# A decoder layer with two head groups: values of the delta rule turned in 32x32 blocks by VectorE, placed by four stores, and scaled by GpSimd after the scan's load

## The chip, the cores and the metric

The kernel runs on one core of one Trainium2 chip, as one launch, in 32-bit floats. The metric is device time in microseconds (us). Before the change the median of three runs is 1235.05 us (1234.37 to 1235.09). The engines are named as the profile names them: PE is TensorE's matmul, PEld its weight load, DVE VectorE, ACT ScalarE, POOL GpSimd, SP SyncE, which issues most of the DMAs.

## What is computed

One decoder layer for 1024 tokens of width 1024. One projection feeds two head groups that work in parallel: group A is differential attention (4 heads), group B a gated delta rule (4 heads, keys and values of 128). Both outputs go through one output projection, and an MLP follows. The change touches the values `v` of group B alone:

```python
dn_qkv = causal_conv_silu(dn_qkv, conv_w[l])
dn_q, dn_k, dn_v = jnp.split(dn_qkv, [DN_HEADS * DN_K_DIM, 2 * DN_HEADS * DN_K_DIM], axis=-1)
...
v_beta = v * beta[..., None]
...
u, w = sol[..., :Dv], sol[..., Dv:]
def step(state, inp):
    q_c, k_c, u_c, w_c, qk_c, g_c = inp
    v_new = u_c - jnp.einsum('bhcd,bhde->bhce', w_c, state)
    o = (jnp.einsum('bhcd,bhde->bhce', q_c * jnp.exp(g_c)[..., None], state)
         + jnp.einsum('bhcj,bhje->bhce', qk_c, v_new))
    ...
```

In words: a causal convolution and SiLU make q, k and v; a triangular system inside each chunk couples the tokens; a scan over chunks carries a 128x128 state for each head.

## The kernel before

All large matmuls are made in three products of rounded halves (hH, hL for the normed input, wH, wL for the weights). The time up to about 350 us runs in these stages.

**Values, keys, queries of the delta rule** (`dn_proj`, L666, up to about 245 us). For each kind (keys, then queries, then values), each head h and each half hf of 512 tokens, TensorE makes a projection `ps_dn` with channels on the partitions and tokens along the free dimension (24 matmuls), ScalarE copies it to `cp`, ScalarE and VectorE do the convolution (`cy`), ScalarE the SiLU. `skew` delays the consumer by one item, so that the next projection is issued first.

The scan wants tokens on the partitions. For the values (loop at L851) `transposed` (L713) therefore sends the four 128x128 tiles of an item through TensorE into PSUM (`ps_t`, L716); VectorE multiplies them by a factor for each token and head (`vsc`, L854) while it moves them to `kn`; `park` (L701) stores the 512x128 result to the DRAM tensor `park_d`, slot 2, in one DMA on SP's queue. `park_d` holds five slots for each head, chunk of 128 tokens and token: raw keys, scaled keys, values, queries and the masked q-k products. The factor `vsc` is made earlier, with the keys (L787, GpSimd).

**The inverse of the triangular system** (`invert`, L743, and `horner`, L797). VectorE inverts 32x32 blocks and sends them through DRAM (`fsg_d`); `horner` loads them into `gb` (L804, sixteen small DMAs for a pair of heads), turns them with a 32x32 block transpose on VectorE (L806), and combines blocks with matmuls `ps_p` (L810) and `ps_h` (L818); `pb` (L813) is a masked copy between them. It is called four times in the value loop, each for a pair of heads and a half.

**The scan** (`scan`, L902), from about 249 to 345 us, interleaved with the projections of group A. It goes through eight chunks. `load` (L907) fetches slots 0 to 2 of a chunk for the four heads into `pka`, four DMAs on SP's queue (L910); `pka` has two buffers, so chunks 0 and 1 are loaded at once and each later load waits until the chunk two before it has been read. `sr` (L922) is values minus keys times state, for chunk 0 the values themselves; then come a matmul with the inverse (L930), a copy `sy` (L932), the state's update (L941, L947) and, in `scan_out` (L956), the chunk's output, which needs slots 3 and 4 (`pkb`, L960).

**Queries, keys and values of group A** (`da_units`, L1041, `da_turns`, L1020) run on TensorE in the same time, one 128-token unit after the other: 24 matmuls `ps_qk` (L1067 to L1069), a norm whose power -1/2 is taken by GpSimd (`rstd`, L288, `rn` at L291), the product `qn` on VectorE (L1092), two transposes `ps_qkt` (L1028, L1029), and a store `qk_d` issued from GpSimd's queue (L1034). When the keys of two heads are stored, `load_head` fetches them (`KS`, L1118) on SP's queue.

**What sets the order.** Within `manual_schedule` and the `Interleave` planner the streams are merged at build time by estimated durations; the tile framework then fixes one order for each engine's queue, also from estimates. On the chip every queue is strictly in order: an instruction that waits for a semaphore holds all that stands behind it on its engine. The same goes for SP's queue of DMAs.

The lines that the change and the prediction touch: the value loop L851 to L857, `park` L701, `load` L907 and its use at L913 and L933; and, beside them on GpSimd's queue, L291, L991 (`mixn_d`), L1034.

Of the kernel before, what the change touches and what calls it, by code (L numbers as in the profile page):

```python
# [13 lines left out]
ALU = mybir.AluOpType  # L14
# [8 lines left out]
NT = SEQ // P  # L23
# [84 lines left out]
def act(n, accum=False):  # L108
    return "S", 55.0 + 0.83 * n + (93.0 if accum else 0.0)


def vec(n, extra=0.0):
    return "V", 68.0 + 1.045 * n + extra


def powr(n):
    return "G", 180.0 + 285.0 * n
# [3 lines left out]
def tile_hymba_layer(  # L121
# [6 lines left out]
    nc = tc.nc  # L128
    V, S, G, T = nc.vector, nc.scalar, nc.gpsimd, nc.tensor
# [40 lines left out]
    park_d = dram.tile([HEADS, NT, P, 5, P], F32, name="park_d")  # L170
# [117 lines left out]
    def rstd(o, ss, scale, eps, pool, tag, n):  # L288
        t = pool.tile([P, n], F32, tag=tag, name=tag) if pool else laid(tag)
        V.tensor_scalar(t, ss, scale, eps, ALU.mult, ALU.add)  # L290
        G.tensor_tensor(o, t, neghalf[:, :n], ALU.pow)  # L291
# [187 lines left out]
    with tc.manual_schedule(engines={T.engine, V.engine, S.engine, G.engine}):  # L479
# [49 lines left out]
        for tb in range(3, NT):  # L529
            for u in range(2):  # L530
                nxt, at = spread_at.get((tb, u), (None, 0))
                z[tb, u] = z_mm(tb, u, *pools[tb], nxt, at)
                if nxt is not None:
# [4 lines left out]
                    if nxt in (4, 5):  # L538
                        b = {4: 5, 5: 7}[nxt]
# [32 lines left out]
    ps = ph.tile([P, 512], F32, tag="ph", name="ps_pv")  # L572
# [24 lines left out]
    v4 = lambda t: t.rearrange("p (c d) -> p c d", d=P)  # L597
# [37 lines left out]
    ps = ph.tile([P, 512], F32, tag="ph", name="ps_g")  # L635
# [21 lines left out]
    def ta(name, bufs, dt=F32):  # L657
        return sa.tile([P, 512], dt, tag=name, name=name, bufs=bufs)

    ssq, ssk, rq, bp, kds, vsc = smalls + [sp.tile([P, 32], F32, name=n) for n in ("kds", "vsc")]  # L660
# [32 lines left out]
    def skew(gen):  # L693
        prev = None
        for it in gen:
            if prev is not None:
                yield prev
            prev = it
        yield prev

    def park(h, hf, slot, src):  # L701
        nc.sync.dma_start(park_d[h, 4 * hf:4 * hf + 4, :, slot, :].rearrange("c p d -> p c d"), v4(src))

    def cols4(t, h, hf):
        return t[:, 8 * h + 4 * hf:8 * h + 4 * hf + 4]

    def bc_col(t):
        return t.unsqueeze(2).broadcast_to([P, 4, P])
# [4 lines left out]
    def transposed(src):  # L713
        ps = pt_.tile([P, 512], F32, tag="pt", name="ps_t")
        for c in range(4):
            T.transpose(ps[:, c * P:(c + 1) * P], src[:, c * P:(c + 1) * P], ident)  # L716
        return ps
# [41 lines left out]
    for h, hf, y, th in skew(dn_proj(1)):  # L759
# [3 lines left out]
        ps = transposed(k2)  # L763
# [65 lines left out]
    for h, hf, q2 in skew(dn_proj(0)):  # L829
# [3 lines left out]
        ps = transposed(q2)  # L833
# [15 lines left out]

    heads = [((h, h + 1), hf) for hf in range(2) for h in (0, 2)]  # L850
    for h, hf, v2 in skew(dn_proj(2)):  # L851
        ps = transposed(v2)
        vs = ta("kn", 2)
        V.tensor_tensor(v4(vs), v4(ps), bc_col(cols4(vsc, h, hf)), ALU.mult)  # L854
        park(h, hf, 2, vs)
        if hf == 0:
            horner(*heads.pop(0))  # L857

# [43 lines left out]
    def scan():  # L902
        St = {}
        psA = pA.tile([P, 512], F32, name="ps_A")
        PA = {h: psA[:, h * P:(h + 1) * P] for h in range(HEADS)}

        def load(c):  # L907
            pka = sb.tile([P, HEADS, 3, P], F32, tag="pka", name="pka", bufs=2)
            for h in range(HEADS):
                nc.sync.dma_start(pka[:, h], park_d[h, c, :, 0:3, :])  # L910
            return pka

        nxt = load(0)  # L913
        for c in range(NT):
            pk, rr_, yy = nxt, {}, {}
            if c > 0:
                for h in range(HEADS):
                    T.matmul(PA[h], pk[:, h, 0, :], St[h], start=True, stop=True)
                for h in range(HEADS):
                    i = cidx(h, c)  # L920
                    rr_[h] = sb.tile([P, P], F32, tag="sr", name="sr", bufs=4)
                    V.scalar_tensor_tensor(rr_[h], PA[h], neg_eg[:, i:i + 1], pk[:, h, 2, :], ALU.mult, ALU.add)  # L922
                flow.pe(4 * MM)
                yield flow.chain(*[vec(P, 60)] * 4), None
            else:
                for h in range(HEADS):
                    rr_[h] = pk[:, h, 2, :]
            for h in range(HEADS):
                Wc = W[h, c // 4][:, (c % 4) * P:(c % 4 + 1) * P]
                T.matmul(PA[h], Wc, rr_[h], start=True, stop=True)  # L930
            y4 = sb.tile([P, 512], F32, tag="sy", name="sy", bufs=2)
            S.copy(y4, psA)  # L932
            if c + 1 < NT:  # L933
                nxt = load(c + 1)
            flow.pe(4 * MM)
            yield flow.chain(act(512)), None
            Sold = dict(St)
            for h in range(HEADS):
                yy[h] = y4[:, h * P:(h + 1) * P]
                if c < NT - 1:  # L940
                    T.matmul(PA[h], pk[:, h, 1, :], yy[h], start=True, stop=True)  # L941
            if c < NT - 1:
                for h in range(HEADS):
                    i = cidx(h, c)
                    Sn = sb.tile([P, P], F32, tag=f"S{h}", name=f"S{h}", bufs=2)
                    if c > 0:
                        V.scalar_tensor_tensor(Sn, St[h], elast[:, i:i + 1], PA[h], ALU.mult, ALU.add)  # L947
                    else:
                        V.tensor_copy(Sn, PA[h])
                    St[h] = Sn  # L950
                flow.pe(4 * MM)
            flow.add(1, scan_out(c, Sold, yy), 0, "pB")
            if c < NT - 1:
                yield flow.chain(*[vec(P, 60)] * 4), None

    def scan_out(c, Sold, yy):  # L956
        pkb = {}
        for h in range(HEADS):
            pkb[h] = sb.tile([P, 2, P], F32, tag="pkb", name="pkb", bufs=5)
            nc.sync.dma_start(pkb[h], park_d[h, c, :, 3:5, :])  # L960
        zgt = sb.tile([P, 512], F32, tag="zgt", name="zgt", bufs=1)
        nc.sync.dma_start(zgt, zg_d[c])
        oc = sb.tile([P, 512], F32, tag="oc", name="oc", bufs=2)
        so = sb.tile([P, 4], F32, tag="so", name="so", bufs=2)
        osq = sb.tile([P, P], F32, tag="osq", name="osq", bufs=1)
        yield flow.now + 2500, "pB"
        if c > 0:
            o1 = pB.tile([P, 512], F32, tag="pB", name="ps_o1")
            for h in range(HEADS):
                T.matmul(o1[:, h * P:(h + 1) * P], pkb[h][:, 0, :], Sold[h], start=True, stop=True)  # L970
            V.tensor_tensor(v4(oc), v4(o1), bc_col(eg[:, c::8]), ALU.mult)
            flow.pe(4 * MM)
            flow.hold("pB", flow.chain(vec(512)))
            yield flow.now, "pB"
        o2 = pB.tile([P, 512], F32, tag="pB", name="ps_o2")
        for h in range(HEADS):
            T.matmul(o2[:, h * P:(h + 1) * P], pkb[h][:, 1, :], yy[h], start=True, stop=True)
        if c > 0:
            V.tensor_tensor(oc, oc, o2, ALU.add)
        else:  # L980
            S.copy(oc, o2)
        for h in range(HEADS):
            i = cidx(h, c)
            S.activation(osq, oc[:, h * P:(h + 1) * P], AF.Square, scale=rq[:, i:i + 1], accum_out=so[:, h:h + 1])
        f = sb.tile([P, 4], F32, tag="of", name="of", bufs=2)
        rstd(f, so, 1.0 / P, EPS, sb, "oft", 4)
        V.tensor_tensor(f, f, rq[:, c::8], ALU.mult)
        for h in range(HEADS):
            V.scalar_tensor_tensor(oc[:, h * P:(h + 1) * P], oc[:, h * P:(h + 1) * P], f[:, h:h + 1],
                                   zgt[:, h * P:(h + 1) * P], ALU.mult, ALU.mult)  # L990
        nc.gpsimd.dma_start(mixn_d[c], oc)  # L991
        flow.pe(4 * MM)
        t = flow.chain(vec(512))
        flow.hold("pB", t)
        flow.chain(*[act(P, True)] * 4, vec(4), powr(4), vec(4), *[vec(P, 60)] * 4, start=t)
        if c == NT - 1:
            s2ctx.close()
            spctx.close()
            mp = ctx.enter_context(tc.tile_pool(name="mp", bufs=1, **left))
            pools["mp"] = mp  # L1000
            for tb in tiles:
                accs[tb] = row_tile("acc")
            pools["a2"] = bctx.enter_context(tc.tile_pool(name="a2", bufs=1, **left))
            pools["be"] = bctx.enter_context(tc.tile_pool(name="be", bufs=2, **left))
            pools["rsc"] = scctx.enter_context(tc.tile_pool(name="rsc", bufs=1, space=PSUM, **right))
            state["scan"] = True
# [911 lines left out]
```

## Time and profile before

| | before |
|---|---|
| median of three runs | 1235.05 us |
| profiled execution | 1234.74 us |
| its span (first to last instruction) | 1233.0 us |
| TensorE busy | 1217.3 us (99%) |
| VectorE busy | 824.7 us (67%) |
| ScalarE busy | 624.2 us (51%) |
| GpSimd busy | 151.3 us (12%) |
| bytes moved by DMA | 202.12 MB |

How to read the rows that follow. A row of a group is: line, engine, operation, out<-in with shapes, count, then busy us and mean ns of one, then the idle time of the engine just before it and what ended it. A row of the timeline is: start in us from the span's start, duration in us, engine (a q behind it is the engine's queue), line, operation, count. A row of a window is: the stretch, its length, then the busy us of PE, PEld, DVE, ACT and POOL with their counts, the granted clock of TensorE, the share of the DMA engines and GB/s. A row of the chain of waits is: start, duration, what. Rows of DMA issues give the KB of each and the median us from issue to landing. Matmul durations overlap, so the cost of one in a stream is read from the distance of the starts.

### The profile page before, as it was taken

What the parts mean: (1) busy time and instruction counts of PE and PEld (TensorE: products, weight loads), DVE (VectorE), ACT (ScalarE), POOL (GpSimd) and SP (SyncE); (2) the same over time, 40 slices, a digit from 0 to 9 for tenths busy, and PEclk for the clock granted to TensorE, in tenths of its full rate; (3) what the DMA queues carried; (4) which work ended last, traced back from release to release, by engine and by line L of the source; (5) the groups of instructions that cost most, each with busy time, mean ns of one, the idle gap of its engine ahead of it and who ended that gap; (6) DMA issues with size and microseconds to landing.
All of it is one profiled execution on the core that took longest, in us unless ns stands there. A gap on an engine that the chain in (4) does not pass through costs nothing.

```text
span 1233.0 us, 18819 instructions
## 1 busy us (share of the span) xinstructions
PE 1217.3 (99%) x6823; PEld 1054.3 (86%) x6823; DVE 824.7 (67%) x1524; ACT 624.2 (51%) x1249; POOL 151.3 (12%) x215
## 2 busy tenths in 40 slices
PE   9999999999999999999999999999999999999998
PEld 8978888898999998888888888888888888888886
DVE  6868796556647657777799544565569755777543
ACT  6588553344346555566666544444564333333330
POOL 2411110043434421001200000000000000000000
PEclk9999999999999999999999999999999999999999
DMA  9344653278748756323437434444479645423301
GB/s 350 98 115 122 163 162 104 63 234 240 231 148 252 232 162 159 85 77 108 157 117 255 172 122 151 171 170 153 155 241 382 234 179 184 163 103 103 137 35 69
DMA packets 143301, 202.12 MB, mean 164 GB/s; under 512 B 20920, under 2 KB 98280, under 8 KB 143208
## 3 DMA queue, kind: packets, MB, share of 16 engines
q1 hardware_dynamic: 138584, 187.28, 46.9%
q0 software_dynamic: 4480, 13.64, 2.9%
q8 instruction: 54, 0.88, 0.3%
q14 instruction: 39, 0.32, 0.1%
q10 hardware_dynamic: 144, 0.00, 0.0%
HBM read 135.86 MB, written 65.01 MB: 163 GB/s over the span
## 4 chain that ended last, share of the span: by engine, by line
PE 88%; DVE 4%; DMA 3%; ACT 2%; issue 2%; POOL 1%; SPq 1%; POOLq 0%; DVEq 0%; ACTq 0%
PE X L1517 4%; PE X L1515 4%; PE X L1516 4%; PE X L1814 4%; PE X L1815 4%; PE X L1813 4%; PE ps_dn L265 3%; PE ps_dn L267 3%; PE ps_dn L266 3%; PE ps_qk L1067 3%; PE ps_qk L1068 3%; PE ps_qk L1069 3%; PE ps_o L1250 2%; PE Y L1515 2%; PE Y L1517 2%; PE Y L1516 2%
## 5 line engine op out<-in xcount | busy, mean ns | idle before, releaser
L1433 ACT CAST hH<-ur 128x1024 fp32r<-128x1024 f32 x56 | 58.9, 1051 | 173.4 <-PE Y L1814 89.8
L1434 DVE TENSOR_TENSOR hL<-ur,hH 128x1024 fp32r<-128x1024 f32 x56 | 68.3, 1223 | 79.4 <-ACT hH L1433 79.4
L1067 PE MATMUL ps_qk<-wH,hH 128*128 128x256 f32 x384 | 114.3, 298 | 0.0
L1069 PE MATMUL ps_qk<-wH,hL 128*128 128x256 f32 x384 | 108.7, 283 | 0.0
L1068 PE MATMUL ps_qk<-wL,hH 128*128 128x256 f32 x384 | 108.4, 282 | 0.0
L1434 DVE TENSOR_TENSOR op<-raw,op 128x1024 fp32r<-128x1024 f32 x48 | 58.7, 1223 | 74.2 <-PE X L1516 41.1
L1813 PE MATMUL X<-hH 128*128 128x512 f32 x224 | 87.1, 389 | 0.0
L1814 PE MATMUL X<-hL,hH 128*128 128x512 f32 x224 | 87.1, 389 | 0.0
L1815 PE MATMUL X<-hH,hL 128*128 128x512 f32 x224 | 87.1, 389 | 0.0
L265 PE MATMUL ps_dn<-hH,wH 128*128 128x512 f32 x192 | 76.3, 397 | 0.2 <-ACT cp L678 0.2
L267 PE MATMUL ps_dn<-hH,wL 128*128 128x512 f32 x192 | 75.8, 396 | 0.0
L266 PE MATMUL ps_dn<-hL,wH 128*128 128x512 f32 x192 | 75.8, 395 | 0.0
L1068 PEld LDWEIGHTS ps_qk<-wL,hH 128*128 128x128 f32 x384 | 73.4, 191 | 0.2
L1067 PEld LDWEIGHTS ps_qk<-wH,hH 128*128 128x128 f32 x384 | 73.3, 191 | 0.2
L1069 PEld LDWEIGHTS ps_qk<-wH,hL 128*128 128x128 f32 x384 | 73.1, 190 | 0.0
L1434 DVE TENSOR_TENSOR hL<-dw,hH 128x1024 fp32r<-128x1024 f32 x56 | 68.2, 1218 | 0.9 <-ACT hH L1433 0.9
L1433 ACT CAST op<-raw 128x1024 fp32r<-128x1024 f32 x48 | 50.4, 1052 | 35.7 <-PE Y L1517 19.9
L1433 ACT CAST hH<-dw 128x1024 fp32r<-128x1024 f32 x56 | 58.7, 1048 | 10.7 <-DMA dw<-in_w_down_dram 5.0
L1205 ACT ACTIVATE pexp<-pexp,mx 128x128 f32<-128x128 f32 (+7 forms) x64 | 49.7, 777 | 25.1 <-DVE mx L1204 24.5
L682 DVE SCALAR_TENSOR_TENSOR cy<-cp,pv,cy 128x512 f32<-128x512 f32 x72 | 53.7, 747 | 8.1 <-ACT cy L680 7.3
L1340 PE MATMUL ps_op<-wH,hH 128*128 128x512 f32 x128 | 53.0, 414 | 0.0
L1515 PE MATMUL Y<-hH,op 128*128 128x512 f32 x128 | 49.9, 390 | 0.4 <-DVE ua L1555 0.4
(370 smaller groups left out, 3429.1 us busy)
## 6 DMA issues: line engine op xcount, KB each, us to landing
ur<-ud SPq DMA_DIRECT2D x28, 1024.0 KB, 5.0
raw<-in_w_up_dram SPq DMA_DIRECT2D x32, 512.0 KB, 3.9
dw<-in_w_down_dram SPq DMA_DIRECT2D x32, 512.0 KB, 6.8
wraw<-in_w_units_dram SPq DMA_DIRECT2D x48, 256.0 KB, 3.7
qk_d<-qa POOLq DMA_DIRECT2D x32, 256.0 KB, 4.3
ud<-ua SPq DMA_DIRECT2D x16, 512.0 KB, 4.2
ud<-s SPq DMA_DIRECT2D x16, 512.0 KB, 2.7
pka<-park_d SPq DMA_DIRECT2D x32, 192.0 KB, 4.8
```

The source lines that it names most:

```text
L265: T.matmul(ps, lh(k), rh(k), start=(k == 0), stop=False)
L266: T.matmul(ps, lh(k), rl(k), start=False, stop=False)
L267: T.matmul(ps, ll(k), rh(k), start=False, stop=(k == n - 1))
L1067: T.matmul(ps[:, :256], hH[:, k, sl], wh[:, k, :], start=(k == 0), stop=False)
L1068: T.matmul(ps[:, :256], hH[:, k, sl], wl[:, k, :], start=False, stop=False)
L1069: T.matmul(ps[:, :256], hL[:, k, sl], wh[:, k, :], start=False, stop=(k == KB - 1))
L1433: S.copy(dst[0], src)
L1434: V.tensor_tensor(dst[1], src, dst[0].bitcast(F32), ALU.subtract)
L1515: T.matmul(ps, op[0][:, k, cs], h[0][:, k, :], start=start and k == 0, stop=False, skip_group_check=True)
L1813: T.matmul(bank[t], v[0][:, j, sl], v[2][:, j], start=s0, stop=False, skip_group_check=True)
L1814: T.matmul(bank[t], v[0][:, j, sl], v[3][:, j], start=False, stop=False, skip_group_check=True)
L1815: T.matmul(bank[t], v[1][:, j, sl], v[2][:, j], start=False, stop=s1, skip_group_check=True)
```

## The change

The values no longer go through TensorE. VectorE turns `v2` in blocks of 32x32 within the 128x512 tile (`V.transpose`), which puts tokens on partitions inside each block but leaves the blocks at their place; four DMAs (`put_blocks`), one for each group of 32 channels, write the blocks to where they belong in `park_d`, in runs of 32 floats. The factor `vsc` is no longer applied there. Instead GpSimd multiplies slot 2 of `pka` by it, in place, after a chunk has been loaded: chunk 0 ahead of the loop, chunk c + 1 at the end of chunk c.

```diff
+    def put_blocks(dst, src):
+
+        for a in range(4):
+            s = slice(32 * a, 32 * a + 32)
+            nc.sync.dma_start(dst[:, s].rearrange("(b s) r -> s b r", s=32),
+                              src[s].rearrange("s (b r) -> s b r", r=32))
...
     for h, hf, v2 in skew(dn_proj(2)):
-        ps = transposed(v2)
         vs = ta("kn", 2)
-        V.tensor_tensor(v4(vs), v4(ps), bc_col(cols4(vsc, h, hf)), ALU.mult)
-        park(h, hf, 2, vs)
+        V.transpose(vs, v2)
+        put_blocks(park_d[h, 4 * hf:4 * hf + 4, :, 2, :].rearrange("c p d -> (c p) d"), vs)
...
+        def scale(c, pk):
+            G.tensor_tensor(pk[:, :, 2, :], pk[:, :, 2, :], bc_col(vsc[:, c::8]), ALU.mult)
+
         nxt = load(0)
+        scale(0, nxt)
         for c in range(NT):
...
             flow.add(1, scan_out(c, Sold, yy), 0, "pB")
+            if c + 1 < NT:
+                scale(c + 1, nxt)
             if c < NT - 1:
                 yield flow.chain(*[vec(P, 60)] * 4), None
```

In the order of the built programs TensorE's queue loses the 32 transposes, and the steps of `horner` stand at other places among the projection matmuls; from the scan's first matmul on, the order on TensorE, VectorE and ScalarE is as before, but for one product `qn` on VectorE that changes places with its neighbour. GpSimd's queue has the eight scalings among its other instructions, SP's has 24 DMAs more.

## The prediction

> **What bounds the kernel now.** I read the head of the page first, then its chain of waits, then the busy time by stretches of 20 us around the two places that the change touches: the values of the delta rule are made from about 185 to 245 us, and the scan loads them from 249 to 320 us.
>
> ```profile
> PE 1217.3 (99%) x6823; PEld 1054.3 (86%) x6823; DVE 824.7 (67%) x1524; ACT 624.2 (51%) x1249; POOL 151.3 (12%) x215
> PE 88%; DVE 4%; DMA 3%; ACT 2%; issue 2%; POOL 1%; SPq 1%; POOLq 0%; DVEq 0%; ACTq 0%
> 200.00:220.00 20.00, 20.00 (x131) 16.62 (x131) 13.88 (x23) 7.99 (x17) 0.00 (x0) 1.00 0.44 117
> 280.00:300.00 20.00, 17.75 (x149) 17.26 (x149) 12.23 (x42) 7.87 (x26) 9.18 (x11) 1.00 0.88 256
> 300.00:320.00 20.00, 19.18 (x166) 18.99 (x165) 13.97 (x42) 9.87 (x31) 6.95 (x9) 1.00 0.83 260
> ```
>
> TensorE is busy 99% of the span and holds 88% of the chain. From 200 to 220 us it has no gap (20.00 of 20.00, granted clock 1.00). So a matmul taken out there is time saved, and a wait put in front of a matmul anywhere is time lost: the order on TensorE is fixed when the kernel is built, and nothing fills the hole. VectorE (13.88 of 20) and GpSimd (0.00 there, 9.18 of 20 in the scan) have room by their busy time. In the scan the DMA engines are the crowded part (0.83 to 0.88).
>
> **What the change takes away.** Eight times four transposes through TensorE (L716 for the values).
>
> ```profile
> 188.67 0.39 PE L266 MATMUL ps_dn<-hL,wH 128*128 128x512 f32 x1
> 188.90 0.39 PE L267 MATMUL ps_dn<-hH,wL 128*128 128x512 f32 x1
> 189.13 0.60 PE L716 MATMUL ps_t<-ident,k 128*128 128x128 f32 x4
> 189.49 0.47 PE L265 MATMUL ps_dn<-hH,wH 128*128 128x512 f32 x1
> 189.80 0.39 PE L266 MATMUL ps_dn<-hL,wH 128*128 128x512 f32 x1
> ```
>
> Undisturbed projection matmuls start 0.23 us apart (188.67, 188.90, 189.13). With the four transposes between, the starts go 189.13, 189.49, 189.80: 0.67 us for what takes 0.23, so a group costs 0.44 us. Eight groups: **-3.5 us**.
>
> **What it puts on VectorE and SP before the scan.**
>
> ```profile
> L854 DVE TENSOR_TENSOR kn<-ps_t,vsc 128x512 f32<-128x512 f32 x8 | 5.4, 678 | 2.6 <-PE ps_t L716 2.6
> L806 DVE STREAM_TRANSPOSE W<-gb 128x512 f32<-128x512 f32 x8 | 5.6, 703 | 1.5 <-DMA gb<-fsg_d 1.4
> L813 DVE TENSOR_TENSOR pb<-ps_p,blk 128x384 f32<-128x384 f32 x8 | 4.3, 541 | 7.5 <-PE ps_p L810 7.5
> q1 hardware_dynamic: 2016, 0.34, 22.2%
> gb<-fsg_d SPq DMA_DIRECT2D x14, 16.0 KB, 1.9
> park_d<-kn SPq DMA_DIRECT2D x16, 256.0 KB, 2.3
> 233.97 9.08 SPq L702 DMA_DIRECT2D park_d<-kn  x2
> 249.42 3.66 SPq L910 DMA_DIRECT2D pka<-park_d  x8
> ```
>
> VectorE gives up eight scalings of 678 ns and takes eight block transposes; the same form stands at L806 with 703 ns. +25 ns each, on an engine that is not the bound: 0.
>
> Each store of 256 KB becomes four of 64 KB, written in runs of 32 floats (128 B). SP issues 24 DMAs more, at some 0.45 us each (the eight pka issues take 3.66 us): 11 us, spread over 50 us of a queue that mostly waits. Behind them in SP's order stand the gb loads of the inverse and weight quarters, moved by one group of stores each (1.3 us); their users come several us later. The transfers: the window with the fourteen gb loads of the same 128 B runs moved 2016 packets in 22.2% of 16 engines' 8.0 us, which is 14 ns a packet. Four stores are 2048 packets, 1.8 us on 16 engines. Before, the last store is issued at the end of the 9.08 us row (242.7) and the scan's first load at 249.42, released by the last pb of L813, not by the store. So 4.4 us are free behind a landing of 2.3. I take 0; bounds 0 and, with 10 us of landing, +3.
>
> [...] No row here shows 128 B stores of this size; 14 ns a packet is from loads. [...]
>
> The order of the built programs shows one more shift: with the transposes gone, the steps of the inverse (L810, L818) move among the projection matmuls, and the last pair runs with nothing between ps_p and the first ps_h. There TensorE sees one pb of 0.54 us that a few matmuls cover now: **+0.5** (bounds 0 and 1.1, two pb).
>
> **What it puts on GpSimd.** Eight scalings of 128x512. Nearest row:
>
> ```profile
> L1370 POOL TENSOR_TENSOR hn<-hn,w2b 128x512 f32<-128x512 f32 x4 | 5.6, 1393 | 6.3 <-ACT hn L1369 6.3
> DMA to landing us min/median/max: 2.4/4.8/6.4
> ```
>
> 1.39 us each; 11 us of a free engine would be nothing. But a scaling waits until its four loads (pka, L910) have landed, the queue is in order, and those loads land late (median 4.8 us). Behind each scaling in GpSimd's new order stand the pow of the QK norm (rn, L291), which VectorE needs for qn and TensorE for the next ps_qkt (L1028), and the stores qk_d (L1034). So I walk through GpSimd's queue as it runs now, put each scaling at its place in the new order, and let it end 1.39 us after its last load landed.
>
> ```profile
> 266.99 0.59 POOL L1034 DMA_DIRECT2D qk_d<-qa  x1 [1.73 <-DVE qa L1033]
> 269.53 1.03 POOL L291 TENSOR_TENSOR rn<-rnt,neghalf 128x4 f32<-128x4 f32 x1
> 280.79 0.60 POOL L1034 DMA_DIRECT2D qk_d<-qa  x1 [5.55 <-DVE rnt L290]
> 286.07 0.54 POOL L1034 DMA_DIRECT2D qk_d<-qa  x1
> 310.90 0.54 POOL L991 DMA_DIRECT2D mixn_d<-oc  x1 [1.31 <-DVE oc L989]
> 311.45 1.03 POOL L291 TENSOR_TENSOR rn<-rnt,neghalf 128x4 f32<-128x4 f32 x1
> 261.94 0.91 SPq L910 DMA_DIRECT2D pka<-park_d  x2
> 271.35 1.85 SPq L910 DMA_DIRECT2D pka<-park_d  x4
> 281.26 1.80 SPq L910 DMA_DIRECT2D pka<-park_d  x4
> 308.23 1.80 SPq L910 DMA_DIRECT2D pka<-park_d  x4
> L910 SPq DMA_DIRECT2D pka<-park_d x2: 430/430/431, 261.9 to 262.4; - x2
> DMA to landing us min/median/max: 5.2/5.4/5.6
> L910 SPq DMA_DIRECT2D pka<-park_d x4: 383/423/430, 308.2 to 309.6; - x4
> DMA to landing us min/median/max: 4.7/5.1/5.5
> L1092 DVE TENSOR_TENSOR qn<-qn,rn 128x256 f32<-128x256 f32 x32 | 13.5, 421 | 7.8 <-POOL rn L291 7.8
> 271.88 0.28 PE L1028 MATMUL ps_qkt<-ident,qn 128*128 128x128 f32 x1
> 313.32 0.31 PE L1028 MATMUL ps_qkt<-ident,qn 128*128 128x128 f32 x1
> 286.07 3.48 DMA qk_d<-qa
> 292.43 6.03 DMA pkb<-park_d
> 298.51 1.18 PE ps_o L970 x6
> ```
>
> - Chunks 0 and 1: the eight loads at 249.42 end their issue at 253.1, the last lands at 252.6 + 4.8 = 257.4, the second scaling ends at 258.8. The third rn, now behind it, then reaches TensorE some 0.6 us after its ps_qkt is due (+0.6; bounds 0 and 2).
> - Chunk 2: last load at 262.4 + 5.6 = 268.0, scaling until 269.4. Its place is ahead of the qk_d of 266.99. Then come that store 0.59, an of of 1.04, a store 0.6, and the rn of 269.53, which now ends at 272.7 in place of 270.6. qn takes 0.42 (L1092), so the ps_qkt of 271.88 starts at 273.2: +1.3.
> - Chunk 3: last load issued at 272.7; with the 5.4 of chunk 2 it lands at 278.1 and the scaling is done at 279.5. GpSimd is idle for 5.55 us ahead of 280.79: 0.
> - Chunk 4: last load issued at 282.6; with 5.0, between the 4.8 of all and the 5.4 here, done at 289.0, ahead of the qk_d of 286.07. That is the store of the last keys of the first head pair; SP waits for its landing (3.48 us) with the KS loads (L1118), and the pkb loads queue behind them on SP. TensorE already waits for pkb at 298.51. All of the delay arrives: 289.0 - 286.07 = +2.95.
> - Chunk 5: by the same steps done at 305.1, ahead of a mixn_d and an rn whose qn has some slack: +0.4.
> - Chunk 6: last load at 309.6 + 5.5 = 315.1, done at 316.5, ahead of the mixn_d of 310.90 and the rn of 311.45. Store 0.54, rn 1.03, qn 0.42 and the hops between: the ps_qkt of 313.32 starts at 318.6: +5.3.
> - Chunk 7: by the same steps +0.4.
>
> Sum of the GpSimd part: 0.6 + 1.3 + 2.95 + 0.4 + 5.3 + 0.4 = **+10.95**. Every such wait moves all later work on TensorE alike, so they add. The scaled values themselves are not late: sr (L922) of a chunk reads them some 8 us after the load landed.
>
> **Sum.** -3.5 + 0.5 + 10.95 = +7.95 us. The profiled execution took 1234.74 us (span 1233.0), 0.3 below the median of 1235.05. Forecast: **1242.7 us**, slower by 0.6%. The measurement of this kernel tells 0.2% (2.5 us) from no change.
>
> The bounds come from the landing of the pka loads, the unknown on which this rests. With 2.4 us for all: chunk 4 costs 1.4 (service alone, behind a mixn_d that ends at 286.07), chunk 6 runs 312.0 to 313.4 and costs 2.2, the others nothing; -3.5 + 3.6 = +0.1, so 1234.8. With 6.4 us: chunks 0 and 1 2.2, chunk 2 2.1, chunk 4 4.3, chunk 5 1.3, chunk 6 6.2, chunk 7 1.0, the tail 1.1: -3.5 + 18.2 = +14.7, so 1249.4.
>
> **Rivals.**
> - The scalings are hidden, and the transposes' gain stands: 1234.74 - 3.5 + 0.5 = 1231.7, faster by 0.25%. For it: chunk 3, whose scaling falls into 5.55 us of idle time; GpSimd is busy for less than half of each stretch. It decides if the loads land within about 2 us of issue, as stores do here (2.3). Against it: no pka load landed faster than 2.4, the DMA engines are at 0.83 and over. 8%.
> - The queue blocks, but the loads land near their minimum, since fewer transfers collide after a stall: the lower bound, 1234.8, no change that can be told. 13%.
> - [...] 7%.
> - The blocked queue costs more than the walk says, because each delayed qk_d store also holds one of two qa buffers and ScalarE then waits for its landing: 2 us more at chunks 2 and 4, with landings near 6.4: 1250 or above. 12%.
>
> The forecast, the walk with landings near those of now, has 60%. Range 1235 to 1249: from the lower bound to the upper one. Chances: faster by over 0.2% 8%, within 0.2% (1232.6 to 1237.5, the second rival and the low end of the forecast) 14%, slower 78%.
>
> **What would show it.** In the changed profile: GpSimd's idle time ahead of the new tensor-tensor on pka, ended by the pka loads, with 2 to 5 us ahead of chunks 2, 4 and 6; TensorE's waits at ps_qkt on qn and at ps_o on pkb, some 10 us more between 250 and 340 us; the value stage to about 245 us some 3 us shorter and free of gaps; the new stores landing in 2 to 3 us. It would be wrong if the scalings start as soon as GpSimd reaches them, if the stretch from 250 to 340 us is no longer than now, or if the 128 B stores or gb loads hold TensorE before 245 us.

## The result, and the profile after

| | before | after |
|---|---|---|
| median | 1234.71 us (1234.28 to 1235.09, 4 runs) | 1242.97 us (1241.18 to 1244.05, 4 runs) |
| ratio | | 1.0066, 95% interval 1.0048 to 1.0083 |
| profiled execution, its span | 1234.74, 1233.0 us | 1244.05, 1242.3 us |
| mean granted clock | 1.000 | 0.996 |

The changed kernel is slower by 8.3 us. First the head of its page (busy time, share, instructions of each engine) and the shares of its chain of waits:

```profile
PE 1218.9 (98%) x6791; PEld 1054.5 (85%) x6791; DVE 826.2 (67%) x1524; ACT 624.3 (50%) x1249; POOL 159.7 (13%) x223
PE 87%; DMA 4%; DVE 3%; ACT 2%; issue 1%; SPq 1%; POOL 1%; POOLq 0%; DVEq 0%; ACTq 0%
```

TensorE has 32 matmuls fewer, yet is busy 1.6 us longer, and GpSimd has 8.4 us of work more: neither says where 9.3 us of span went. The stretches of 20 us do (length, then PE, PEld, DVE, ACT, POOL busy with their counts, granted clock, DMA share, GB/s):

```profile
280.00:300.00 20.00, 16.02 (x135) 15.45 (x134) 11.30 (x39) 7.54 (x26) 10.06 (x12) 1.00 0.81 224
300.00:320.00 20.00, 15.19 (x121) 14.73 (x122) 12.10 (x36) 6.85 (x20) 8.75 (x11) 0.96 0.75 253
320.00:340.00 20.00, 19.76 (x149) 19.41 (x148) 10.34 (x30) 7.18 (x22) 7.52 (x11) 0.87 0.51 165
```

Against the rows of before, TensorE is idle 1.7 us more in 280 to 300 and 4.0 us more in 300 to 320. In 320 to 340 it is as busy as before (19.76 both times), but at a granted clock of 0.87. A busy row alone would hide that loss; the clock column shows it.

Next, GpSimd's order of events around chunks 4 and 6 (start, duration, what; in brackets the idle time before it and what ended it). L920 is the new scaling, L291 the pow:

```profile
287.94 1.04 POOL L920 TENSOR_TENSOR pka<-pka,vsc 128x512 f32<-128x512 f32 x1 [2.33 <-DMA pka<-park_d]
288.94 0.58 POOL L1046 DMA_DIRECT2D qk_d<-qa  x1
289.54 1.03 POOL L291 TENSOR_TENSOR rn<-rnt,neghalf 128x4 f32<-128x4 f32 x1
...
315.80 1.04 POOL L920 TENSOR_TENSOR pka<-pka,vsc 128x512 f32<-128x512 f32 x1 [3.06 <-DMA pka<-park_d]
316.79 0.58 POOL L1003 DMA_DIRECT2D mixn_d<-oc  x1
317.39 1.03 POOL L291 TENSOR_TENSOR rn<-rnt,neghalf 128x4 f32<-128x4 f32 x1
```

GpSimd stands idle 2.33 and 3.06 us for a load, and the store and the pow come right behind the scaling: they were ready and had to wait. The waits of TensorE from 255 to 340 us (in total, times, longest), first after, then before:

```profile
PE ps_qkt L1040 <- DVE qn L1104: 8.0, 6, 3.5
PE ps_o L982 <- DMA pkb<-park_d: 1.3, 1, 1.3
```

```profile
PE ps_qkt L1028 <- DVE qn L1092: 1.3, 2, 1.0
PE ps_o L970 <- DMA pkb<-park_d: 1.2, 1, 1.2
```

The wait for qn grew by 6.7 us. The chain of waits of after, between 282 and 320 us, links the two pictures (start, length, what held the chain):

```profile
282.55 5.22 DMA pka<-park_d
287.94 0.48 POOL pka L920
...
288.94 2.38 DMA qk_d<-qa
...
294.19 6.25 DMA pkb<-park_d
300.49 1.17 PE ps_o L982 x6
...
310.74 4.89 DMA pka<-park_d
315.80 0.48 POOL pka L920
...
316.79 0.58 POOL mixn_d L1003
317.39 1.04 POOL rn L291
318.46 0.44 DVE qn L1104
318.94 0.48 PE ps_qkt L1040
```

Such a load is on the critical chain twice, though the scan needs it only some 10 us later (chunk 4's values are read by sr at 299 us): GpSimd waits for it with other engines' work behind it.

Last, TensorE's own rows at chunk 6 and the clock in steps of 2 us:

```profile
315.17 0.28 PE L1081 MATMUL ps_qk<-wH,hL 128*128 128x256 f32 x1
318.94 0.48 PE L1040 MATMUL ps_qkt<-ident,qn 128*128 128x128 f32 x1 [3.49 <-DVE qn L1104]
...
319.28 0.56 PE L1079 MATMUL ps_qk<-wH,hH 128*128 128x256 f32 x1
319.64 0.41 PE L1080 MATMUL ps_qk<-wL,hH 128*128 128x256 f32 x1
```

```profile
316.00:318.00 2.00, 0.00 (x0) 0.00 (x0) 0.39 (x2) 0.00 (x0) 1.98 (x3) 1.00 0.37 119
318.00:320.00 2.00, 1.06 (x5) 1.06 (x6) 0.50 (x2) 0.33 (x1) 1.32 (x2) 0.55 0.31 117
320.00:322.00 2.00, 2.00 (x12) 2.00 (x11) 0.82 (x2) 0.14 (x1) 0.72 (x2) 0.50 0.00 0
322.00:324.00 2.00, 2.00 (x11) 2.00 (x11) 0.00 (x0) 0.06 (x1) 0.00 (x0) 0.50 0.34 131
324.00:326.00 2.00, 2.00 (x15) 2.00 (x15) 0.56 (x1) 0.52 (x1) 0.00 (x0) 0.74 0.27 83
```

After 3.49 us of idle time TensorE came back at half its clock: the same matmul takes 0.41 us in place of 0.28, and 2 us hold 12 matmuls in place of 19. Full speed returns at about 325 us. This part was in no step of the prediction.

The stretch can be booked at the ps_qkt transposes, which stand in the same order in both kernels. Their lead (-) or lag (+) against before, in us, from the two traces:

| | before | after | lag | step |
|---|---|---|---|---|
| first ps_dn, ahead of everything changed | 58.84 | 59.48 | +0.64 | +0.64 |
| 1st ps_qkt, end of the value stage | 253.19 | 251.29 | -1.90 | -2.54 |
| 3rd, past chunks 0 and 1 | 259.77 | 258.93 | -0.84 | +1.06 |
| 6th, past chunk 2 | 271.88 | 271.40 | -0.48 | +0.36 |
| 9th, at chunk 4 | 289.33 | 291.18 | +1.85 | +2.33 |
| 12th, past chunk 5 | 307.01 | 308.99 | +1.98 | +0.13 |
| 13th, at chunk 6 | 313.32 | 318.94 | +5.62 | +3.64 |
| 15th, past the half clock | 324.70 | 333.28 | +8.58 | +2.96 |
| end of the span | 1233.0 | 1242.3 | +9.3 | +0.7 |

The first and the last row (1.3 us together) lie outside what was changed; the profiled execution is also the longest of its four, 1.1 us above their median.

### The profile page after: what moved, and what is told of

Read it like the earlier page. It is cut to its first block, busy times and chain, and to the rows that moved or that the text cites. A ratio compares the mean times of both kernels' runs of the same rounds, so it can differ in the third digit from the quotient of the medians.

```text
span 1242.3 us, 18801 instructions
## 1 busy us (share of the span) xinstructions
PE 1218.9 (98%) x6791; PEld 1054.5 (85%) x6791; DVE 826.2 (67%) x1524; ACT 624.3 (50%) x1249; POOL 159.7 (13%) x223
## 4 chain that ended last, share of the span: by engine, by line
PE 87%; DMA 4%; DVE 3%; ACT 2%; issue 1%; SPq 1%; POOL 1%; POOLq 0%; DVEq 0%; ACTq 0%
PE X L1529 4%; PE X L1527 4%; PE X L1528 4%; PE X L1827 4%; PE X L1826 4%; PE X L1825 4%; PE ps_dn L265 3%; PE ps_dn L267 3%; PE ps_dn L266 3%; PE ps_qk L1079 3%; PE ps_qk L1081 3%; PE ps_qk L1080 3%; PE Y L1527 2%; PE ps_o L1262 2%; PE Y L1528 2%; PE Y L1529 2%
## 5 line engine op out<-in xcount | busy, mean ns | idle before, releaser
L1354 PE MATMUL ps_op<-wH,hL 128*128 128x512 f32 x128 | 50.3, 393 | 0.0
```

## The experiments

Each was timed beside the kernel before on its chip. Those chips gave 1235.65 to 1236.13 us for it, about 1 us more than the first one and with more scatter, so I compare differences.

**e1: no scaling.** The two calls of `scale` are gone, so the values enter the scan without their factor `vsc`.

> The changed kernel without the eight scalings of the loaded values (the factor vsc is left out of the computation). My theory: all of the loss comes from GpSimd waiting, in order, for the loads that it scales. Then only the value stage remains, which in the profiled run was 2.6 us shorter (start of the first values' matmuls to the scan): 1232.1 us, between 1231.0 and 1233.5, no TensorE wait of over 1 us at ps_qkt between 285 and 326 us, granted clock 1.00 throughout. Rival, the 24 more stores with their runs of 128 B and their issues on SP cost something in the scan: 1236 or more.

Measured 1234.48 us against 1235.71, ratio 0.9992 (0.9983 to 1.0001): 1.2 us below, where the theory had 2.6; the interval reaches 1, so it is not shown to be faster than before. The loss is gone with the scalings, so the stores carry none of it that can be told. But the saving does not arrive in full. The trace says where it went: the 9th ps_qkt is still 1.8 us ahead of before, the 11th 0.4, the 13th 0.4 behind. TensorE's waits from 245 to 350 us:

```profile
PE ps_o L979 <- DMA pkb<-park_d: 2.3, 1, 2.3
PE ps_qkt L1037 <- DVE qn L1101: 1.9, 3, 1.0
```

TensorE arrives earlier at a load that does not come earlier (1.2 us of wait before, 2.3 here), and after that wait the clock was at 0.50 from 297.9 to 301.3 us, against the theory's 1.00. In this trace a saving ahead of a transfer that is late anyway is paid back there.

**e2: the scaling issued a step later in the source.**

```diff
-        scale(0, nxt)
         for c in range(NT):
             pk, rr_, yy = nxt, {}, {}
+            scale(c, pk)
             if c > 0:
...
-            if c + 1 < NT:
-                scale(c + 1, nxt)
```

> The scaling of chunk c stays on GpSimd with its 1.05 us, but is issued at the start of chunk c, some 10 us after its load was issued, not at the end of chunk c-1, some 2 us after. My theory (head of the queue blocked by a load on its way): GpSimd finds the data landed, 1232 to 1234 us, and its idle time ahead of pka ended by pka loads falls from 19.2 us to under 4. Rival (the work itself on GpSimd, eight times 1.05 us, delays rn and qk_d or the sr that waits for it): 1238 to 1242.

Measured 1243.49 us against 1235.71, ratio 1.0063 (1.0050 to 1.0075): 7.8 us above, no gain. The edit missed its aim. GpSimd's rows at chunk 4:

```profile
288.78 1.04 POOL L920 TENSOR_TENSOR pka<-pka,vsc 128x512 f32<-128x512 f32 x1 [2.73 <-PE ps_qk L1079]
289.77 0.58 POOL L1044 DMA_DIRECT2D qk_d<-qa  x1
290.37 1.03 POOL L291 TENSOR_TENSOR rn<-rnt,neghalf 128x4 f32<-128x4 f32 x1
```

The profile puts the 2.73 us down to PE, but the last load of this chunk was issued at 283.1 us and took 5.5, so it landed at 288.6: GpSimd waited for the load. The order is that of the changed kernel, here and in the rest of the scan, though the call stands elsewhere in the source. That the framework's estimate has the load landed by then, and so leaves the instruction where it was, is my reading; no run shows it. So e2 tested nothing but served as a repetition on another chip: +7.8 beside +8.3.

**e3: the same on VectorE** (`V.tensor_tensor` in `scale`).

> As e2, but the scaling stands on VectorE (128x512, some 0.7 us by the 678 ns of the form that the change removed). My theory: 1232 us plus what sr comes later for seven chunks, 0 to 0.7 us each, so 1232 to 1236 us and GpSimd as before the change. If VectorE's order were what bounds the scan: over 1237.

Measured 1250.46 us against 1235.71, ratio 1.0118 (1.0104 to 1.0132): 14.8 us above, far over the theory's 1236 and worse than on GpSimd. VectorE's longest wait from 245 to 350 us:

```profile
DVE pka L920 <- DMA pka<-park_d: 17.4, 6, 4.6
```

The scalings stand ahead here too (chunk 2's comes before the sr of chunk 1), so a busier engine stood waiting for the loads, and three of TensorE's waits were followed by half clock. That it is the work on VectorE which costs is not shown, since the place was not the one intended; that the blocked head of a queue costs more the more stands behind it fits.

**e4: the scalings alone**, with the values turned by TensorE and parked by one store, as before.

```diff
+        ps = transposed(v2)
         vs = ta("kn", 2)
-        V.transpose(vs, v2)
-        put_blocks(park_d[h, 4 * hf:4 * hf + 4, :, 2, :].rearrange("c p d -> (c p) d"), vs)
+        V.tensor_copy(vs, ps)
+        park(h, hf, 2, vs)
```

> The GpSimd scalings of the change alone: the values go through TensorE's transposes as before, are copied unscaled by VectorE and parked by one store of 256 KB each. My theory: the loss is the whole of the change's scalings, and the value path gives 2.6 us: 1243.0 + 2.6 = 1245.6 us (1243.5 to 1248). Rival (the small stores and their issues carry part of the loss): 1240 or less.

Measured 1245.49 us against 1235.71, ratio 1.0071 (1.0058 to 1.0084): 9.8 us above. The loss belongs to the scalings; the rival for the small stores falls. By the medians the rest of the change gives 1.5 to 2 us (against +8.3, and +7.8 in e2), but the intervals overlap. At chunk 6 the wait for qn is again 3.49 us, with the clock at half behind it, but the half clock lasted 3.4 us here and cost 1.55 (the lag against before grows from 8.05 at the 13th ps_qkt to 9.60 at the 15th), where it cost 2.96 in the changed kernel.

**e5: another place in the queue.** The scalings of chunks 1, 2, 4, 5 and 6 are issued at the start of their own chunk and pinned behind a pow that stood behind them (`pows` collects the pow instructions of rn in their order).

```diff
+    pows, behind = [], {1: 4, 2: 6, 4: 10, 5: 12, 6: 14}
...
+            if c in behind:
+                with tc.issue_after(pows[behind[c] - 1].ins):
+                    scale(c, pk)
...
-            if c + 1 < NT:
+            if c + 1 < NT and c + 1 not in behind:
                 scale(c + 1, nxt)
```

> All eight scalings on GpSimd, but those of chunks 1, 2, 4, 5 and 6 are queued behind the pow (rn) of a QK tile that stood behind them before: the 4th, 6th, 10th, 12th and 14th. Same instructions, same loads, another place in GpSimd's queue. My theory (the place in the queue ahead of rn and qk_d, not the work): TensorE's waits at ps_qkt for qn fall from 8.0 us to under 2.5, and the time is that of the kernel without scalings, 1.5 us below to 1 us above the kernel before. Rival (the 1.05 us of work each, or a scan that then waits for its values): 4 us or more above the kernel before.

Measured 1238.46 us (1235.53 to 1241.43) against 1235.65, ratio 1.0021 (1.0011 to 1.0032): 2.8 us above, between the two expectations. Two thirds of the loss go with the same eight scalings on the same engine, which rules out their work as the cause of that part; but it is not the time of e1, and the waits for qn fall to 3.3 us, not under 2.5. TensorE's waits, and the row where the longest ends:

```profile
PE ps_qkt L1045 <- DVE qn L1110: 3.3, 4, 1.4
PE ps_o L987 <- DMA pkb<-park_d: 2.9, 1, 2.9
PE ps_A L945 <- POOL pka L922: 0.6, 1, 0.6
```

```profile
298.21 1.65 PE L987 MATMUL ps_o<-S,pkb 128*128 128x128 f32 x6 [2.85 <-DMA pkb<-park_d]
```

The scan's waits for its own scaled values are 0.6 us in all. The longest that is left is the pkb wait of e1, with half clock behind it again (granted clock 0.77 and 0.81 in 296 to 300 and 300 to 304 us). As e1 has that wait too, it does not account for the 4 us between the two. In their traces e5 falls behind e1 in small steps: 0.8 us at the 3rd ps_qkt, 0.7 at the 6th, 0.7 at the pkb wait, 0.7 at the 13th.

**e6: chunk 6 alone** pinned (`behind` is `{6: 14}`).

> As the changed kernel, but the scaling of chunk 6 alone is queued behind the 14th rn. The changed kernel stands 8.3 us above the kernel before; its wait there was 3.5 us, and the stretch at half clock behind it cost 2.7 us. My theory (wait and clock are one event): both go, some 6 us, so 1 to 4 us above the kernel before and granted clock 1.00 from 300 to 335 us. If the clock drop has another cause: about 4.8 us above. If the wait only moves to the next load: 6 or more above.

Measured 1238.52 us against 1235.65, ratio 1.0023 (1.0014 to 1.0032): 2.9 us above, in the range of the theory. The wait at the 13th ps_qkt falls from 3.49 to 0.48 us. The clock is not at 1.00 from 300 to 335 us, though: in this execution it was the pkb wait, 3.17 us, that was followed by half speed. Moving one instruction past two pows is worth some 5 us.

**e7: the wait filled with work.** At chunk 6, behind the last ps_qk matmul (`newest["PE"]`), TensorE gets 28 matmuls whose result the transposes overwrite.

```diff
             pt = bank_tile(px, r, "ps_qkt")
+            if state["turned"] == 12:
+                with tc.issue_after(newest["PE"].ins):
+                    for j in range(28):
+                        T.matmul(pt[:, 0:256], hH[:, 0, 0:P], hH[:, 1, 0:256], start=True, stop=True)
```

> The changed kernel with 28 matmuls more (128x256, 0.12 us apart, 3.4 us in all, their result is overwritten) on TensorE in the wait of chunk 6, between the last ps_qk and the transposes of the 13th qn. The wait stays, TensorE is no longer idle in it. My theory (the clock falls because TensorE idled for over 3 us): transposes at the same time as before within 0.4 us, granted clock 1.00 from 314 to 330 us, and the time falls by the 2.7 us of the half clock: 4.5 to 7 us above the kernel before. Rival (the clock falls for another reason, or the extra work costs as much): 8 us or more above, with rows of 0.5.

Measured 1241.21 us against 1235.65, ratio 1.0048 (1.0036 to 1.0060): 5.6 us above, where the kernel without the 28 matmuls is 8.3 above. TensorE's rows, and the clock:

```profile
315.76 3.52 PE L1043 MATMUL ps_qkt<-hH 128*128 128x256 f32 x28
319.15 0.33 PE L1044 MATMUL ps_qkt<-ident,qn 128*128 128x128 f32 x1
```

```profile
318.00:320.00 2.00, 2.00 (x18) 1.93 (x17) 0.50 (x2) 0.37 (x1) 1.32 (x2) 1.00 0.35 131
320.00:322.00 2.00, 2.00 (x20) 2.00 (x19) 0.82 (x2) 0.15 (x2) 0.85 (x2) 1.00 0.00 0
```

The transposes start at 319.15 us (318.94 without), the clock stays at 1.00, and the next ps_qkt follows 5.09 us later, where it took 7.90 in the changed kernel and 5.07 before. In that trace the 2.8 us of the half clock are the price of having idled, apart from the idle time itself.

**e8, e9, e10: the keys out of the way.** The KS loads wait for GpSimd's store of the last keys (4.2 us in e5), and the pkb loads stand behind them on SP (issued from 291.12 us there, right after the four KS loads that start at 288.31). They are queued behind the last pka load:

```diff
-        heads[0] = load_head(0, ap), load_v(0, ap)
+        with tc.issue_after(newest["pka"].ins):
+            heads[0] = load_head(0, ap), load_v(0, ap)
```

> As e5, and the loads of the first head's keys (KS, first used some 75 us later) are queued on SP behind the last pka load, so that the pkb loads of chunk 4 no longer stand behind loads that wait for a store of GpSimd. In e1, e5 and e6 TensorE waited 2.3 to 3.2 us for those pkb loads, and the clock was halved behind it. My theory: that wait was what ate the 2.6 us which the value stage saves; with it gone the kernel is 1 to 3.5 us below the kernel before, with no row of granted clock under 1.00 between 250 and 345 us. Rival (the DMA engines are full there, whatever the order): the wait stays over 2 us, and the time at that of e5, 0 to 3 us above the kernel before.

> The kernel before with the same move of the KS loads and nothing else. Its wait for the pkb loads was 1.2 us, with the clock at 1.00: 0 to 1.5 us below the kernel before. If e8 is below this one, the change is worth having once its scalings and the keys are placed; if not, all of the gain belongs to the keys.

> The changed kernel with the same move of the KS loads, the scalings where the change put them. My prediction laid chunk 4's loss on the chain from the last store of the keys over KS and pkb to ps_o: its wait of 1.3 us at ps_o goes, that of 2.1 us at ps_qkt for qn stays, and so does chunk 6 with its half clock: 6 to 7.5 us above the kernel before. If the KS loads were the cause of chunk 4's and chunk 5's delay as a whole: 5 us or less. If they were not in the way: 8 us or more.

| | measured | before | ratio (95%) |
|---|---|---|---|
| e8: e5 and the keys | 1233.76 us | 1235.86 | 0.9985 (0.9976 to 0.9994) |
| e9: before and the keys | 1234.32 us | 1235.86 | 0.9990 (0.9981 to 0.9999) |
| e10: after and the keys | 1243.05 us | 1235.86 | 1.0061 (1.0049 to 1.0074) |

All three are where the theory had them, e9 at the end of its range (1.5 us below). e8 is 2.1 us below the kernel before, with no wait at ps_o left; its waits from 245 to 350 us and the whole stretch of the scan:

```profile
PE ps_qkt L1045 <- DVE qn L1110: 3.2, 5, 1.1
PE ps_A L945 <- POOL pka L922: 0.2, 1, 0.2
```

```profile
250.00:345.00 95.00, 91.56 (x776) 90.03 (x776) 61.63 (x179) 41.93 (x124) 46.97 (x57) 1.00 0.75 234
```

e10 shows how little a gain is worth ahead of a fixed event. At the 11th ps_qkt it is 2.4 us ahead of the changed kernel (301.52 against 303.91), but at the 13th only 1.2, since the wait for chunk 6's load grew from 3.49 to 4.64:

```profile
317.69 0.48 PE L1040 MATMUL ps_qkt<-ident,qn 128*128 128x128 f32 x1 [4.64 <-DVE qn L1104]
```

**e11, e12: e8 and e9 once more**, for what the change is worth when its scalings and the keys are placed well.

> The kernel of e8 once more beside that of e9, on one chip, for the question whether the change is worth having once its scalings and the keys are placed: e8 was 0.56 us below e9 in the median of eleven runs each, 1.9 us in the time of the profiled runs' ps_qkt transposes at 325 us. If the value path keeps what it saves (2.6 us less about 1.2 of small waits): 1 to 2 us below e12 again. If it doesn't: within 0.6 us of it.

> The kernel of e9 once more: 1.0 to 2.0 us below the kernel before, as in e9 (1.5).

Measured 1234.19 us (ratio 0.9984, 0.9975 to 0.9993) and 1234.90 us (0.9987, 0.9978 to 0.9996), against 1236.13. The two medians differ by 0.7 us, between the two expectations, by 0.6 in the first pair; the means over both pairs, 22 runs each, by 0.5 with a 95% interval of about 0.7 to either side. So the best version of the change is not shown to be faster than the kernel before with its keys moved. Both are faster than the kernel before, by 0.1 to 0.2%.

## Why the prediction was right, step by step

The forecast was 1242.7 us, the median 1242.97. The mechanism was the one named, and e4, e5 and e6 show it: queue positions on GpSimd, not work and not stores. For two thirds of the loss that is measured (e5); what keeps e5 above e1 is seen only as small waits. But that the sum is right to 0.3 us is luck: two errors cancel, the waits were over-priced by 3.4 us, and the clock was left out, by 3.0. Of the "some 10 us more" of waits at ps_qkt and ps_o that were to show it, 6.8 came.

- *The transposes and the tail*, -3.0 in the sum: -2.54 in the table. The projection runs without the gap that was priced (starts at 188.81, 189.04, 189.27 in the changed trace, 0.23 apart). Size off by 0.5. The tail's +0.5 did not show: no matmul waits for pb, and from 185 to 249 us TensorE is idle for 0.33 us in all (0.47 before). So it is the transposes that gave less than 3.5. (The upper bound leaves out the +0.5 of the forecast; with it, it is 1249.9.)
- *VectorE's transposes*, 0: TensorE shows no new wait there. *The small stores*, 0: they land in 2.0 us and the first pka load is issued at 248.18, earlier than before (249.42).

```profile
park_d<-kn SPq DMA_DIRECT2D x32, 64.0 KB, 2.0
248.18 4.61 SPq L916 DMA_DIRECT2D pka<-park_d  x8
```

  That is the row which the prediction lacked for 128 B runs. From 185 to 249 us the DMA engines are busy for 0.41 of the time at 83 GB/s, where the kernel before, with its large stores, has 0.29 at 80. That it is the small pieces which cost more fits; what makes them dearer no row shows. But nothing waits for that, and e1 and e4 find no loss in the time.
- *The scaling*, priced at 1.39 us by another tensor-tensor: 1.04 to 1.05 us, once 1.29 (chunk 5). A third of a microsecond too much in every chunk but one. The 1.39 was a mean of four with one of 1.71 in it; their median is 1.29.
- *Chunks 0 and 1, 2, 5, 7*: forecast 0.6, 1.3, 0.4, 0.4. Steps of the table: 1.06, 0.36, 0.13, and nothing that can be told for chunk 7. Ahead of chunk 5 GpSimd stood idle for 4.55 us, longer than at chunk 6, and TensorE lost next to nothing: what counts is who waits behind.
- *Chunk 4*: forecast 2.95 by way of qk_d, KS, pkb and ps_o; 2.33 came. The chain of waits runs as said, but TensorE first stopped at the 9th ps_qkt, for the pow that also stood behind the scaling (2.13 us), a second path that the walk did not name. The lag was taken there; the wait at ps_o is 1.30 us where it was 1.21. e10 cuts the first: with the keys away the 9th ps_qkt still waits 1.77 us.
- *Chunk 6*: forecast 5.3, came 3.64. The path (rn, qn, ps_qkt) is right. The scaling was shorter by 0.34, the last load landed in 4.89 us rather than 5.5, and it was issued at 310.74, 1.1 us later than before, while TensorE was 2.0 later. Here the sentence that failed is "they add": a lag that TensorE has already got makes the next wait for a load shorter. e10 is the same from the other side.
- *What was missing*: the price of idling. The sum took an idle microsecond as a microsecond. At chunk 6 it cost 1.8 (3.64 and 2.96). That this matched the over-priced waits is chance: the same wait in e4 cost 1.55 behind it.

Of the rivals, the hidden scalings are refuted by the rows above. The 7% was my chance for small stores that land late: no run shows late ones, those of the changed kernel landed in 1.8 to 3.8 us. "Loads near their minimum" (2.4 us) did not come: chunk 4's four landed in 5.2 us, chunk 6's in 4.0 to 4.9. The cascade over the qa buffers was not seen as a wait of its own.

One thing the forecast did not see at all, since the scalings covered it: most of the saving ahead of the scan is paid back at the pkb loads (1.4 of 1.8 us in the trace of e1). Its first rival had priced hidden scalings at a gain of 3.0 us; without any scaling the gain is 1.2, not clear of noise.

## What to carry to other kernels

Before moving work to an engine that looks idle, list what will stand behind it in that engine's queue: an instruction that waits for a transfer lends its wait to everything behind it, however little work it is itself (here 1.04 us of work behind 3.06 us of waiting at chunk 6). Check the built queue and not the source order, and pin the instruction behind the urgent ones if the framework's order has it ahead of them. And read the granted clock beside the idle time: the stall of 3.49 us cost 1.8 times its length in one kernel and 1.4 times in another (e4).

## What the runs showed of the hardware

The clock after an idle stretch of TensorE, from the rows of the profiled runs, in the scan's stretch from 245 to 350 us (half clock is where the 128x256 matmuls that follow take 0.41 us, full where they take 0.28):

| idle us | half clock after it | full clock after it |
|---|---|---|
| 1.38 to 1.80 | none | 1.38 (e5), 1.75 (e6), 1.77 (e10), 1.80 (e7) |
| 1.87 to 2.85 | 1.87 and 2.08 (e3), 2.26 (e1), 2.85 (e5) | 1.96 (e7), 2.13 (after), 2.18 and 2.52 (e2) |
| 3.17 to 4.64 | 3.17 (e6), 3.49 (after, e4), 4.25 (e2), 4.34 (e3), 4.64 (e10) | none |

The gaps from 1.87 to 2.85 us went both ways; the six from 3.17 us on were all followed by half clock. Here are the rows around the 1.87 us of e3, and those around the 2.52 of e2 (length, then the busy time of PE first; the clock is the third number from the end):

```profile
338.00:340.00 2.00, 0.21 (x3) 0.21 (x3) 2.00 (x7) 0.00 (x0) 0.00 (x0) 1.00 0.08 31
340.00:341.00 1.00, 1.00 (x10) 1.00 (x9) 1.00 (x3) 0.48 (x1) 0.00 (x0) 1.00 0.77 205
341.00:342.00 1.00, 1.00 (x7) 1.00 (x6) 1.00 (x6) 0.00 (x0) 0.43 (x1) 0.53 0.51 127
342.00:343.00 1.00, 1.00 (x7) 1.00 (x6) 1.00 (x5) 0.37 (x1) 1.00 (x2) 0.50 0.44 143
```

```profile
288.00:294.00 6.00, 3.48 (x31) 3.30 (x30) 1.89 (x6) 1.21 (x3) 3.86 (x5) 1.00 0.25 96
294.00:300.00 6.00, 6.00 (x53) 5.80 (x51) 3.08 (x11) 3.45 (x12) 1.89 (x3) 1.00 1.11 248
```

The half clock did not always last equally long. My estimate, from the granted clock of the window rows (twice what a row lacks to 1.00, times its length): 3.4 to 3.5 us in e1, e2, e4, e5 and twice in e3, and 6.8 us in the changed kernel (its rows of 318 to 326 us) and behind the 4.34 of e3. What decides whether a gap is followed by half clock, and for how long, is not shown; no experiment changed the length or the place of a gap alone. What e7 shows is that with 28 matmuls in the wait of chunk 6 the clock stayed at 1.00.

A tensor-tensor of 128x512 took 1.04 to 1.05 us on GpSimd in seven of the eight scalings of the changed kernel and 1.29 in one; in the row of the MLP (L1370) by which it had been priced the median is 1.29. What makes the difference is open.
